# Masks by one whole number per column, stores on their makers' queues, first heads' values apart, output weights in four buffers, logs grouped

## Chip, cores, metric

One core of one Trainium2 chip runs the whole program. The metric is the device time of one execution in microseconds (us); the number compared is the median over several runs.

## What is computed

One layer of a hybrid encoder block on 1024 tokens of width 1024, all in float32:

```python
proj = h @ w_in[l]                                  # one projection for everything below
aq, ak, av, iq, ik, iw, bq, bk, bv, br, bg = split(proj)
# sparse attention, 8 heads of 64: an index score picks 256 keys per query
rel   = relu(einsum('bqhd,bsd->bqhs', iqb, ik))     # 8 index heads of 32
score = einsum('bqhs,bqh->bqs', rel, iwb)           # -inf for later chunks of 64
vals, idx = top_k(score, 256)                       # ties: the lower key first
p  = softmax(qb . k[idx] * 64**-0.5);  ya = p . v[idx]
# gated linear attention, 4 heads: decay from log_sigmoid(bg @ w_gate + b) / 16
log_a = log_sigmoid(bg @ w_gla_gate + b_gla_gate) / 16
b = cumsum(log_a) per chunk;  qg = q*exp(b);  kg = k*exp(-b);  ...
yb = rms_norm(o) * g * silu(br)
h = layer_norm(alpha*h + concat(ya, yb) @ w_out)
# mixture of 32 experts (4 groups of 8), top 2 inside the best group
h = layer_norm(alpha*h + hier_moe(h))
```

## The kernel before

Every float32 product is done as three products of rounded parts: a tensor x becomes `hi` (x rounded) and `lo` (x - hi), and TensorE (PE) sums hi*hi, hi*lo and lo*hi in PSUM. `split` makes the pair: ScalarE (ACT) copies `hi`, VectorE (DVE) or GpSimd (POOL) subtracts.

The work goes in stages. **Input phase** (`in_phase`): x^T is loaded and split into eight `big` tiles; index queries and keys and the first half of the attention's values (`values(0, ...)`) are projected, rotated and written to HBM scratch. `decays` makes the gates' logs: a matmul on the `g` PSUM banks, an exponential (L539), a logarithm with its subtraction (L542, L543), then a matmul with a triangle of ones that sums them (L547) and two exponentials of the sums, stored to `d_decay` (L552, L553). `index_scores` goes over query tiles t = 2 to 7 of 128 rows: for each of 8 index heads a matmul (L477), a Relu on ACT (L478) and a weighted accumulation on DVE (L484, L486). After each head it takes steps from `rest`, a generator of the linear attention's projections (`gla_inputs`); `BETWEEN` says how many units per head, one entry for each t. What is left of `rest` runs afterwards. A unit is one accumulation step (three matmuls) of a 256-column product; steps of a 512-column one count two.

**Queries and keys, threshold search, linear attention** run side by side. `queries_keys` projects (L221), rotates (DVE L264 to L267, POOL L268 and L269), splits (`split_out`) and stores queries and keys (`d_q`, `d_k`, L279 and L280). `topk_phase` finds the 256th largest score of each row by a search over the 31 bits of a float: four of the six columns (the query tiles 2 to 7, 384 to 1024 keys wide) are counted on DVE (L709), the two widest on ACT (L739). Then each column gets a mask in `bias`: the sign of score minus threshold (ACT L764), the ties (L765), a running count of them (L766), how many ties are still wanted (L768, L769), the wanted ties (L770), their sum with the sign on POOL (L771), and the comparison that writes 0 or -1e30 (L772). `values(1, ...)` projects the other half of the values at the end of this stage (L674 copies, L675 stores to `d_av`). `gla_phase` does the linear attention in four halves, stored through `ym` to `d_mix` (L664, L665).

**Attention** (`attention`): 32 items, four pairs of heads times eight query tiles, software-pipelined by hand: scores (L817), masked maximum (DVE L822), exponential (ACT L830), transposes (L841) copied to `PT` (L844, L846), product with the values (L855), normalization (POOL copy L888, transpose L863, L866) and store to `d_mix` (L867). `attention_loads` fetches queries, keys and values of a pair: for pair 0 into four tiles `kq0` to `kq3` of the pool `first_qk`, for the others into the `big` tiles that held x. Values of pairs 0 and 1 are loaded together into `kq3`, those of 2 and 3 into one `big` tile. At item 8 `first_qk` is closed, and the output weights' tiles `wolo`, `woraw`, `wohi` are opened over it: `load_wout` fetches a raw piece, `split_wout` splits it on POOL (L930, L931), one of 16 pieces after each of the items 8 to 23.

**Output projection** (`out_phase`): eight token tiles; each loads its mixed rows `mraw` (L1001; they share the `woraw` buffers) and the old x, multiplies by the split output weights (L1019), normalizes and routes. The first pieces of the experts' weights are loaded between (`next_raw`, L949). **Experts**: 32 experts in turn, 192 weight pieces of 1 MB streamed through 13 slots, split on ACT and DVE (L179, L180), multiplied (L1230), results added to `d_y` by an indirect DMA (L1279). A last normalization ends the kernel.

The order on each engine comes from the framework's scheduler, which plans with its own costs, except where `manual_schedule` or `issue_after` fixes it. Each engine runs its instructions in that order. A DMA is issued from a queue: SP's, ACT's or POOL's; the issue stands in that engine's order and waits there for what it needs. SP's queue carries nearly all DMAs.

Of the kernel before, what the change touches and what calls it, by code (L numbers as in the profile page):

```python
# [46 lines left out]
BETWEEN = (1, 1, 1.5, 1.5, 2, 2)  # L47
# [116 lines left out]
class Kern:  # L164
# [107 lines left out]
    def split_out(self, pool, src, dst_hi, dst_lo, lo_eng):  # L272

        nc = self.nc
        m, n = src.shape
        hi = pool.tile([128, 512], F32R, name="so_hi", bufs=2)[:m, :n]
        lo = src.bitcast(F32R)
        self.split(hi, lo, src, lo_eng)
        nc.sync.dma_start(dst_hi, hi.bitcast(F32))  # L279
        nc.sync.dma_start(dst_lo, lo.bitcast(F32))  # L280


    def run(self):
        tc, nc, I = self.tc, self.nc, self.I
        with ExitStack() as ctx:
# [34 lines left out]
            with ExitStack() as ps:  # L320
# [3 lines left out]
                with self.pool("att") as ap:  # L324
# [3 lines left out]
                    loads = [self.attention_loads(0, [fq.tile([128, 2, D], F32R if i < 3 else F32, name=f"kq{i}") for i in range(4)], nc.scalar)]  # L328

                    def more():  # L330
                        hp = len(loads)
                        loads.append(self.attention_loads(hp, [self.big(F32R) for _ in range(3)] + ([self.big()] if hp == 2 else [])))

                    def before(n):
# [3 lines left out]
                        if n == 8:  # L338
# [6 lines left out]
                            for q in range(2):  # L345
                                self.load_wout(wl, q)
# [19 lines left out]
    def in_phase(self, gla):  # L366
        tc, nc, I = self.tc, self.nc, self.I
        with ExitStack() as ctx:
# [6 lines left out]
            with self.pool("first") as fp:  # L375
# [23 lines left out]
                with self.pool("idx") as p:  # L399
# [10 lines left out]
                    self.decays(p)  # L410
# [4 lines left out]
                    self.index_scores(p, rest)  # L415
# [3 lines left out]
            with self.pool("qk") as p, self.pool("topk", side="right") as tp:  # L419
# [3 lines left out]
                self.all_of(self.values(1, self.load_w(I["wi"][P_AV + 1], 256), (0, 2, 4, 6)))  # L423
# [27 lines left out]
    def index_scores(self, p, rest):  # L451
# [13 lines left out]
        for t in range(2, NT):  # L465
            W = WS[t - 2]
# [54 lines left out]
    def decays(self, p):  # L521
# [7 lines left out]
        for hp, h in halves:  # L529
# [9 lines left out]
            nc.scalar.activation(u, u, AF.Exp)  # L539
            logs.append((u, loga))  # L540
        for u, loga in logs:
            nc.scalar.activation(u, u, AF.Ln, bias=1.0)  # L542
            nc.gpsimd.tensor_tensor(loga, loga, u, op=OP.subtract)  # L543
        for (hp, h), (u, loga) in zip(halves, logs):
# [4 lines left out]
            for k, tag in enumerate(("u", "loga")):  # L549
                e = p.tile([128, 512], F32, name=f"e{k}", tag=tag, bufs=4)  # L550

                nc.scalar.activation(e, bp, AF.Exp, scale=(0.0625, -0.0625)[k])  # L552
# [46 lines left out]
    def gla_half(self, p, hp, h, S, operands, AT, causal):  # L599
# [50 lines left out]
        for hd in range(2):  # L650
# [14 lines left out]
            nc.sync.dma_start(self.d_mix[h][:, :, 4 + 2 * hp + hd, :].rearrange("t p q -> p t q"), ym)  # L665
# [3 lines left out]
    def values(self, g, w, tiles):  # L669
        nc = self.nc  # L670
        for t in tiles:
# [3 lines left out]
            nc.sync.dma_start(self.d_av[g][:, :, t:t + 2, :].rearrange("a p t c -> p a t c"), vs)  # L675

    def queries_keys(self, p):
# [5 lines left out]
        for g in range(2):  # L683
            for n, dst in enumerate((self.d_q[g], self.d_k[g])):
                w = self.load_w(I["wi"][P_AQK + 2 * g + n], 256)
                for h in range(2):
# [4 lines left out]
                    for i in range(2):  # L691
                        o = dst[:, :, 32 * i:32 * i + 32, ts]
                        self.split_out(p, r[i], o[:, 0], o[:, 1], nc.gpsimd)


    def topk_phase(self, p):
# [4 lines left out]
        jnk = p.tile([128, T], BF, name="sn", bufs=1)  # L701
# [56 lines left out]
        for i in range(n):  # L758
            W = WS[i]

            sn = p.tile([128, T], BF, name="sn", bufs=1)[:, :W]
# [742 lines left out]
```

## Time and profile before

| | us |
|---|---|
| median of the 3 runs shown (1343.27 to 1349.84) | 1346.22 |
| the profiled execution's own time | 1340.77 |
| its span in the profile | 1339.0 |
| PE busy in the span | 1218.8 (91%) |
| DVE busy | 1016.0 (76%) |
| ACT busy | 801.1 (60%) |
| POOL busy | 385.5 (29%) |

Times in the profile count from the start of the span. Busy is the union of an engine's instructions. Matmuls overlap each other, so a busy PE is not always PE at its peak: many short ones at a low granted clock mean that it waits. The chain of waits is followed back from the last instruction; 67% of it lies on PE. "Idle before" an instruction names what ended the wait, by inference from semaphore events.

### The profile page before, as it was taken

The numbers are of one execution on the slowest core, as the hardware profiler recorded it, in microseconds if no ns is written. First come the engines' busy times: TensorE is split into PE (matmuls) and PEld (weight loads), VectorE is DVE, ScalarE is ACT, GpSimd is POOL, SyncE is SP. The second block draws the span as 40 slices with busy tenths as digits, with TensorE's granted clock in tenths as the row PEclk, the third lists the DMA queues.
The fourth block names the chain that finished last, engine by engine and source line by source line (L and its number), as shares of the span: only waits on it lengthen the run. The fifth ranks groups of instructions, "written<-read, shape, count | busy, mean of one in ns | idle before, by whom it ended". The sixth has DMA issues, their size and how long they took to land.

```text
span 1339.0 us, 19330 instructions
## 1 busy us (share of the span) xinstructions
PE 1218.8 (91%) x6894; PEld 1011.5 (76%) x6894; DVE 1016.0 (76%) x1646; ACT 801.1 (60%) x1117; POOL 385.5 (29%) x340
## 2 busy tenths in 40 slices
PE   7979999999994999499967999999999999999962
PEld 5967988977793887388856888888888888888841
DVE  4537888999854666256675999999999999999855
ACT  5487366665413666222244787777778777777735
POOL 3422532344652025411121212212222221222124
PEclk9988999999996999799968999999999999999985
DMA  7554434224366742567338999999999999999926
GB/s 250 160 166 139 127 127 141 95 74 143 110 192 181 204 111 65 211 231 260 138 112 314 335 371 371 382 375 368 366 367 373 354 354 350 358 357 347 352 55 251
DMA packets 130004, 322.57 MB, mean 241 GB/s; under 512 B 15577, under 2 KB 46194, under 8 KB 129906
## 3 DMA queue, kind: packets, MB, share of 16 engines
q1 hardware_dynamic: 114802, 287.73, 60.9%
q0 software_dynamic: 10496, 21.00, 6.1%
q10 hardware_dynamic: 4608, 12.58, 2.6%
q8 instruction: 55, 0.90, 0.3%
q14 instruction: 43, 0.35, 0.1%
HBM read 283.77 MB, written 54.26 MB: 252 GB/s over the span
## 4 chain that ended last, share of the span: by engine, by line
PE 67%; DMA 13%; DVE 9%; ACT 4%; issue 3%; POOL 2%; SPq 0%; ACTq 0%; POOLq 0%; DVEq 0%
PE acc L1230 23%; PE ot L1230 11%; PE acc L1019 7%; PE acc L235 6%; PE acc L221 4%; DVE eq L709 3%; PE pt L1293 3%; PE s L817 3%; PE ot L855 2%; DMA d_y<-y,tok 2%; PE pt L841 2%; DMA slot<-we 2%; PE g L221 2%; DMA big<-wf 2%; PE ot L1046 1%
## 5 line engine op out<-in xcount | busy, mean ns | idle before, releaser
L180 DVE TENSOR_TENSOR elo<-big,ehi 128x2048 fp32r<-128x2048 f32 (+1 forms) x132 | 268.1, 2061 | 22.2 <-ACT ehi L179 21.0
L179 ACT CAST ehi<-big 128x2048 fp32r<-128x2048 f32 (+1 forms) x132 | 223.1, 1724 | 3.8 <-DMA big<-we 2.5
L1230 PE MATMUL acc<-ehi,xh 128*128 128x512 f32 x512 | 206.5, 403 | 4.7 <-ACT sg L1342 4.7
L1230 PE MATMUL acc<-elo,xh 128*128 128x512 f32 x512 | 203.3, 397 | 0.3 <-DVE elo L180 0.3
L1230 PE MATMUL acc<-ehi,xl 128*128 128x512 f32 x512 | 203.2, 397 | 0.3 <-DVE xl L180 0.3
L1300 POOL DMA_INDIRECT xg<-d_h,tok x32 | 37.4, 1169 | 372.9 <-PE pt L1293 370.5
L235 PE MATMUL acc<-whi,big 128*128 128x256 f32 x736 | 136.5, 285 | 0.4 <-ACT rel L478 0.4
L221 PE MATMUL acc<-big,whi 128*128 128x512 f32 (+1 forms) x384 | 120.8, 394 | 9.7 <-ACT big L179 9.7
L1279 POOL DMA_INDIRECT d_y<-y,tok x32 | 92.8, 2900 | 100.5 <-DVE y L1278 40.6
L1230 PEld LDWEIGHTS acc<-ehi,xh 128*128 128x128 f32 x512 | 97.3, 190 | 26.5 <-ACT sg L1342 5.1
L235 PEld LDWEIGHTS acc<-whi,big 128*128 128x128 f32 x736 | 115.4, 191 | 2.4 <-issue 0.9
L1230 PEld LDWEIGHTS acc<-ehi,xl 128*128 128x128 f32 x512 | 97.1, 190 | 23.9 <-DVE xl L180 1.0
L1230 PEld LDWEIGHTS acc<-elo,xh 128*128 128x128 f32 x512 | 97.3, 190 | 22.5 <-DVE elo L180 1.2
L709 DVE TENSOR_SCALAR_CACHE_REDUCE eq<-sc,cand 128x384 bf16<-128x384 f32 (+1 forms) x124 | 100.5, 810 | 5.9 <-POOL sc L721 3.4
L235 PE MATMUL acc<-wlo,big 128*128 128x256 f32 x368 | 104.7, 285 | 0.0
L1230 PE MATMUL ot<-ehi,ah 128*128 128x512 f32 x256 | 103.6, 405 | 0.4 <-ACT ah L179 0.4
L180 DVE TENSOR_TENSOR elo<-slot,ehi 128x2048 fp32r<-128x2048 f32 (+1 forms) x46 | 95.5, 2101 | 9.5 <-ACT ehi L179 9.1
L1230 PE MATMUL ot<-ehi,al 128*128 128x512 f32 x256 | 101.1, 395 | 0.1
L1230 PE MATMUL ot<-elo,ah 128*128 128x512 f32 x256 | 101.0, 394 | 0.0
L1019 PE MATMUL acc<-wohi,m 128*128 128x512 f32 x256 | 84.1, 405 | 18.0 <-ACT m L179 18.0
L739 ACT ACTIVATE sn<-sc,cand 128x896 bf16<-128x896 f32 (+1 forms) x62 | 67.9, 1095 | 48.5 <-DVE cand L735 46.2
L221 PEld LDWEIGHTS acc<-big,whi 128*128 128x128 f32 x384 | 73.0, 194 | 25.5 <-ACT big L179 9.7
(288 smaller groups left out, 2565.5 us busy)
## 6 DMA issues: line engine op xcount, KB each, us to landing
big<-we SPq DMA_DIRECT2D x79, 1024.0 KB
big<-wf SPq DMA_DIRECT2D x40, 1024.0 KB
slot<-we SPq DMA_DIRECT2D x26, 1024.0 KB
sc<-we SPq DMA_DIRECT2D x20, 1024.0 KB
slot<-wf SPq DMA_DIRECT2D x16, 1024.0 KB
wraw<-wi SPq DMA_DIRECT2D x52, 256.0 KB
sc<-wf SPq DMA_DIRECT2D x8, 1024.0 KB
raw<-xT SPq DMA_DIRECT2D x8, 512.0 KB
```

The lines of the kernel that those rows point to most:

```text
L179: nc.scalar.copy(hi, src)
L180: (lo_eng or nc.vector).tensor_tensor(lo, src, hi.bitcast(F32), op=OP.subtract)
L221: nc.tensor.matmul(ps[:m, :n], l[:, j, c0:c0 + m], r[:, j % 2, t0:t0 + n], start=(j == 0 and a == 0), stop=(j == 7 and a == 2))
L235: nc.tensor.matmul(ps[:, i, :], l[:, j % 2, s], r[:, j, :], start=(j == 0 and a == 0), stop=(j == 7 and a == 2))
L709: nc.vector.tensor_scalar(gtt[:, :WS[i]], x, v, 0.0, op0=op, op1=OP.add, accum_out=cnt[:, i:i + 1])
L739: nc.scalar.activation(jnk[:, :WS[i]], y[i], AF.Sign, bias=c, accum_out=cnt[:, i:i + 1])
L817: nc.tensor.matmul(ps[:, 512 * c:512 * c + mm], lq, kk[hd][:, a, c0:c0 + mm], start=a == 0, stop=a == 1)
L1019: nc.tensor.matmul(ps, l[:, j, :], w[:, j, s], start=(j == 0 and a == 0), stop=(j == 7 and a == 2))
L1230: nc.tensor.matmul(o, x[:, jj, :], w[:, j, s], start=(jj == 0 and a == 0), stop=(jj == n - 1 and a == 2))
L1279: nc.gpsimd.indirect_dma_start(out=self.d_y, out_offset=bass.IndirectOffsetOnAxis(ap=tok.bitcast(U32), axis=0), in_=y, in_offset=None, bou ...
L1293: self.last_mm = nc.tensor.transpose(pt[:, 128 * i:128 * i + 128], src[:, 128 * (b + i):128 * (b + i) + 128], self.c["ident"])
L1300: self.last_gather = nc.gpsimd.indirect_dma_start(out=xg, out_offset=None, in_=self.d_h, in_offset=bass.IndirectOffsetOnAxis(ap=tok.bitcas ...
```

## The change

- **Masks.** Per column, DVE now forms 1024*sign - running count in the 16-bit float `pre` and compares it with one number per row, `need`, that says how many ties are taken. POOL's add goes. `sn` gets two buffers.
- **Stores.** In `queries_keys` the high part goes out from ACT's queue and the low part from POOL's; `values(1, ...)` and the linear attention's `ym` store from ACT's queue. All were on SP's.
- **First heads.** `attention_loads(0)` moves from ACT's queue to SP's. `kq3` holds the values of pair 0 alone and is half as large; pair 1 gets its values in a `big` tile of its own.
- **Output weights.** `woraw` has four buffers instead of two; the 16 pieces go by column half first and by row block second.
- **Logs.** `decays` ends after the logarithms, which are tied behind the last exponential on ACT; sums and their exponentials become `decay_sums`, called before query tile 5 in `index_scores` and tied behind the last logarithm. The last two entries of `BETWEEN` rise from 2 to 4.

```diff
-BETWEEN = (1, 1, 1.5, 1.5, 2, 2)
+BETWEEN = (1, 1, 1.5, 1.5, 4, 4)
+WORAW = 4
...
-    def split_out(self, pool, src, dst_hi, dst_lo, lo_eng):
+    def split_out(self, pool, src, dst_hi, dst_lo, lo_eng, queues=None):
...
-        nc.sync.dma_start(dst_hi, hi.bitcast(F32))
-        nc.sync.dma_start(dst_lo, lo.bitcast(F32))
+        q = queues or (nc.sync, nc.sync)
+        q[0].dma_start(dst_hi, hi.bitcast(F32))
+        q[1].dma_start(dst_lo, lo.bitcast(F32))
...
-                    loads = [self.attention_loads(0, [fq.tile([128, 2, D], F32R if i < 3 else F32, name=f"kq{i}") for i in range(4)], nc.scalar)]
+                    slots = [fq.tile([128, 2, D], F32R, name=f"kq{i}") for i in range(3)] + [fq.tile([128, D], F32, name="kq3")]
+                    loads = [self.attention_loads(0, slots)]
...
-                        loads.append(self.attention_loads(hp, [self.big(F32R) for _ in range(3)] + ([self.big()] if hp == 2 else [])))
+                        loads.append(self.attention_loads(hp, [self.big(F32R) for _ in range(3)] + ([self.big()[:, 0]] if hp == 1 else [self.big()] if hp == 2 else [])))
...
-                            for q in range(2):
+                            for q in range(WORAW):
                                 self.load_wout(wl, q)
...
-                    self.decays(p)
+                    logs = self.decays(p)
...
-                    self.index_scores(p, rest)
+                    self.index_scores(p, rest, lambda: self.decay_sums(p, *logs))
...
-                self.all_of(self.values(1, self.load_w(I["wi"][P_AV + 1], 256), (0, 2, 4, 6)))
+                self.all_of(self.values(1, self.load_w(I["wi"][P_AV + 1], 256), (0, 2, 4, 6), nc.scalar))
...
         for t in range(2, NT):
+            if t == 5:
+                between()
...
-            nc.scalar.activation(u, u, AF.Exp)
+            last = nc.scalar.activation(u, u, AF.Exp)
             logs.append((u, loga))
-        for u, loga in logs:
-            nc.scalar.activation(u, u, AF.Ln, bias=1.0)
-            nc.gpsimd.tensor_tensor(loga, loga, u, op=OP.subtract)
+        with self.tc.issue_after(last.ins):
+            for u, loga in logs:
+                last = nc.scalar.activation(u, u, AF.Ln, bias=1.0)
+                nc.gpsimd.tensor_tensor(loga, loga, u, op=OP.subtract)
+        return halves, logs, last
+
+    def decay_sums(self, p, halves, logs, last):
+        nc = self.nc
         for (hp, h), (u, loga) in zip(halves, logs):
...
-                nc.scalar.activation(e, bp, AF.Exp, scale=(0.0625, -0.0625)[k])
+                with self.tc.issue_after(last.ins):
+                    nc.scalar.activation(e, bp, AF.Exp, scale=(0.0625, -0.0625)[k])
...
-            nc.sync.dma_start(self.d_mix[h][:, :, 4 + 2 * hp + hd, :].rearrange("t p q -> p t q"), ym)
+            nc.scalar.dma_start(self.d_mix[h][:, :, 4 + 2 * hp + hd, :].rearrange("t p q -> p t q"), ym)
...
-                        self.split_out(p, r[i], o[:, 0], o[:, 1], nc.gpsimd)
+                        self.split_out(p, r[i], o[:, 0], o[:, 1], nc.gpsimd, (nc.scalar, nc.gpsimd))
...
-        jnk = p.tile([128, T], BF, name="sn", bufs=1)
+        jnk = p.tile([128, T], BF, name="sn", bufs=2)
...
-            sn = p.tile([128, T], BF, name="sn", bufs=1)[:, :W]
+            sn = p.tile([128, T], BF, name="sn", bufs=2)[:, :W]
...
+            nc.vector.tensor_scalar(need[:, i:i + 1], cnt[:, i:i + 1], 0.5, 0.5 * W - TOPK, op0=OP.mult, op1=OP.add)
             nc.vector.tensor_scalar(eq, sn, 0.0, None, op0=OP.is_equal)
             nc.vector.tensor_tensor_scan(pre, eq, eq, 0.0, op0=OP.add, op1=OP.max)
-            nc.vector.tensor_scalar(need[:, i:i + 1], cnt[:, i:i + 1], -0.5, TOPK - 0.5 * W, op0=OP.mult, op1=OP.add)
-            nc.vector.scalar_tensor_tensor(need[:, i:i + 1], pre[:, W - 1:W], 0.5, need[:, i:i + 1], op0=OP.mult, op1=OP.add)
-            nc.vector.scalar_tensor_tensor(eq, pre, need[:, i:i + 1], eq, op0=OP.is_le, op1=OP.mult)
-            nc.gpsimd.tensor_tensor(sn, sn, eq, op=OP.add)
-            nc.vector.tensor_scalar(self.bias[i + 2], sn, 0.0, NEG, op0=OP.is_le, op1=OP.mult)
+            nc.vector.scalar_tensor_tensor(need[:, i:i + 1], pre[:, W - 1:W], -0.5, need[:, i:i + 1], op0=OP.mult, op1=OP.add)
+            nc.vector.scalar_tensor_tensor(pre, sn, 1024.0, pre, op0=OP.mult, op1=OP.subtract)
+            nc.vector.tensor_scalar(self.bias[i + 2], pre, need[:, i:i + 1], NEG, op0=OP.is_lt, op1=OP.mult)
...
-    def attention_loads(self, hp, slots, queue=None):
+    def attention_loads(self, hp, slots):
...
-            if hp % 2 == 0:
-                queue.dma_start(self.vv.rearrange("p a (t c) -> p a t c", c=128)[:, :, 4 * th:4 * th + 4],
-                                  self.d_av[hp // 2][:, :, 4 * th:4 * th + 4].rearrange("a p t c -> p a t c"))
+            if hp < 2:
+                nc.sync.dma_start(self.vv.rearrange("p (t c) -> p t c", c=128)[:, 4 * th:4 * th + 4], d_av[hp][:, 4 * th:4 * th + 4])
...
-        raw = p.tile([128, 512], F32, name="woraw", tag="woraw", bufs=2)
-        s = slice(512 * (q % 2), 512 * (q % 2) + 512)
+        raw = p.tile([128, 512], F32, name="woraw", tag="woraw", bufs=WORAW)
+        s = slice(512 * (q // 8), 512 * (q // 8) + 512)
...
-        if q + 2 < 16:
-            self.load_wout(p, q + 2)
+        if q + WORAW < 16:
+            self.load_wout(p, q + WORAW)
...
-                raws = [self.wor.tile([128, 4, 128], F32, name="mraw", tag="woraw", bufs=2) for _ in range(2)]
+                raws = [self.wor.tile([128, 4, 128], F32, name="mraw", tag="woraw", bufs=WORAW) for _ in range(2)]
```

More of the change, by code (lines that the diff above doesn't have):

```diff
@@ L449, in index_keys, with index_scores @@
             self.split_out(p, r[i], dk[i, :, ts], dk[2 + i, :, ts], nc.vector)
-    def index_scores(self, p, rest):
+    def index_scores(self, p, rest, between):
         nc, I = self.nc, self.I
@@ L664, in gla_half, with values @@
             nc.scalar.copy(ym.rearrange("p a b -> p (a b)"), tps)
-            nc.sync.dma_start(self.d_mix[h][:, :, 4 + 2 * hp + hd, :].rearrange("t p q -> p t q"), ym)
+            nc.scalar.dma_start(self.d_mix[h][:, :, 4 + 2 * hp + hd, :].rearrange("t p q -> p t q"), ym)
         return S
-    def values(self, g, w, tiles):
+    def values(self, g, w, tiles, queue=None):
         nc = self.nc
+        queue = queue or nc.sync
         for t in tiles:
@@ L674, in values @@
             nc.scalar.copy(vs, ps.rearrange("p t (a b) -> p a t b", a=2))
-            nc.sync.dma_start(self.d_av[g][:, :, t:t + 2, :].rearrange("a p t c -> p a t c"), vs)
+            queue.dma_start(self.d_av[g][:, :, t:t + 2, :].rearrange("a p t c -> p a t c"), vs)
     def queries_keys(self, p):
@@ L775, in topk_phase @@
         nc.vector.tensor_copy(self.bias[1][:, 128:256], self.c["diag"])
-    def attention_loads(self, hp, slots, queue=None):
-        queue = queue or self.nc.sync
-        d_q, d_k, h0 = self.d_q[hp // 2], self.d_k[hp // 2], 2 * (hp % 2)
+    def attention_loads(self, hp, slots):
+        nc = self.nc
+        d_q, d_k, d_av, h0 = self.d_q[hp // 2], self.d_k[hp // 2], self.d_av[hp // 2], 2 * (hp % 2)
         qq, kk = slots[0], slots[1:3]
-        if hp % 2 == 0:
+        if len(slots) > 3:
             self.vv = slots[3]
@@ L919, in load_wout @@
     def load_wout(self, p, q):
[L921 to L923 removed]
+        raw = p.tile([128, 512], F32, name="woraw", tag="woraw", bufs=WORAW)
+        s = slice(512 * (q // 8), 512 * (q // 8) + 512)
+        self.nc.gpsimd.dma_start(raw, self.I["wo"].rearrange("(j p) c -> p j c", p=128)[:, q % 8, s])
         self.woraw.append(raw)
     def split_wout(self, p, q):
[L927 to L928 removed]
+        s = slice(512 * (q // 8), 512 * (q // 8) + 512)
+        hi, lo = self.wohi[:, q % 8, s], self.wolo[:, q % 8, s]
         raw = self.woraw[q]
```

16 lines of the change are left out of this document (8 added, 8 removed).

## Prediction

> **What bounds the kernel now.** I read the page first: TensorE (PE) is the busiest engine by far, so a part beside a full PE can pay nothing. I then cut the span into stages (busy time of each engine by window) to find where PE stands still, and read each engine's timeline, the list of waits and the chain of waits around those places.
>
> ```profile
> 70.00:85.00 15.00, 7.85 (x37) 6.39 (x35) 0.18 (x1) 14.50 (x23) 6.45 (x6) 0.66 0.36 122
> 85.00:119.00 34.00, 33.91 (x178) 29.51 (x179) 22.68 (x29) 22.94 (x49) 7.62 (x8) 1.00 0.49 146
> 119.00:137.40 18.40, 16.52 (x40) 8.38 (x38) 17.15 (x17) 15.66 (x33) 1.70 (x4) 0.72 0.49 151
> 137.40:407.00 269.60, 266.83 (x1818) 232.40 (x1818) 228.86 (x619) 139.20 (x295) 126.22 (x107) 0.99 0.40 127
> 407.00:430.20 23.20, 4.65 (x18) 3.42 (x18) 7.23 (x25) 5.32 (x14) 5.00 (x3) 0.54 0.72 194
> 430.20:548.20 118.00, 113.78 (x1071) 94.95 (x1070) 71.01 (x180) 76.89 (x174) 34.62 (x46) 0.99 0.46 124
> 548.20:566.20 18.00, 0.04 (x1) 0.04 (x1) 0.75 (x2) 1.20 (x2) 8.38 (x10) 0.61 0.90 332
> ...
> 726.00:1275.00 549.00, 548.82 (x2543) 448.42 (x2544) 497.98 (x348) 413.36 (x346) 118.00 (x59) 1.00 0.99 359
> ```
>
> Columns: window, its length, busy time of PE, PE's weight loads, VectorE (DVE), ScalarE (ACT) and GpSimd (POOL) with instruction counts, granted clock, DMA share, GB/s. Four windows have a hole: 70 to 85 (the gate logs), 7.2 us without PE work and a clock of 0.66; 119 to 137.4 (the last two index-score tiles), where 40 matmuls spread over 16.5 us at 0.72; 407 to 430.2 (start of the attention), 4.65 busy of 23.2; 548.2 to 566.2 (start of the output projection), 0.04 of 18.0. Between them PE is full: 266.83 of 269.6 us from 137.4, 548.82 of 549 in the experts. The change can win in these holes only.
>
> **Hole 1: the logs.**
>
> ACT's timeline (start us, length us, line, operation), and PE's row, whose bracket is the idle time before it:
>
> ```profile
> 61.89 1.28 ACT L542 ACT_TABLE_LOAD   x1
> 63.19 0.63 ACT L542 ACTIVATE u<-u 128x512 f32<-128x512 f32 x1
> ...
> 75.49 1.28 ACT L552 ACT_TABLE_LOAD   x1
> 76.79 1.08 ACT L552 ACTIVATE e<-g 128x512 f32<-128x512 f32 x2
> ```
>
> ```profile
> 77.97 2.05 PE L547 MATMUL g<-Kin,loga 128*128 128x128 f32 x8 [6.23 <-issue]
> ```
>
> ACT alternates exponential and logarithm with a table load of 1.28 us each time: eight from 61.89 to 75.49. PE stands 6.23 us until the last sums of the logs. The change ties all logarithms behind the last exponential and the later exponentials behind the last logarithm: two loads, six fewer, 6 x 1.28 = 7.7 us of ACT. It also puts the sums (four groups of eight matmuls, eight exponentials of 0.54 us, their stores) behind the third index tile, so no score queues behind them. PE gets back 7.2 us, and of the 7.85 us busy at clock 0.66 some 2 to 3 us. Against that, 8 x 0.54 + 1.28 = 5.6 us of ACT move into the score stage. ACT has 11 of 34 us free from 85 to 119, which hides them; in the last two tiles it has 2.7 us free, and then up to 5.6 us show. I take 8 gained, ends 3 and 10.
>
> ScalarE: Activation LUTs of the Trainium skill, "Table sets: the hidden batching unit", says that exponential and logarithm lie together in one set, so that going from one to the other needs no second load. By that rule grouping would save no load, and the sum would be 36 us instead of 44; the trace does not agree, it has a load of 1.28 us at each alternation.
>
> **Hole 2: the last score tiles.**
>
> PE's timeline, and a window in which it runs 256-column matmuls almost alone:
>
> ```profile
> 119.43 1.73 PE L477 MATMUL acc<-K,Q 128*128 128x384 f32 x6
> ...
> 128.23 8.76 PE L477 MATMUL acc<-K,Q 128*128 128x512 f32 x16 [0.36 <-ACT rel L478]
> ```
>
> ```profile
> 154.00:180.00 26.00, 26.00 (x212) 25.70 (x211) 21.63 (x56) 13.36 (x24) 20.34 (x15) 1.00 0.47 148
> ```
>
> These rows are the first and last of the stretch in which PE holds scores alone. Its matmuls need at most 0.23 us each at full clock (512 columns, twice the 256 below), 7 to 8 us; about 11 are unused. DVE (17.15 of 18.4) and ACT (15.66) pace it. The raised last entries of BETWEEN feed two more projection steps after each of 16 heads: 32 steps of three 256-column matmuls at 26.0/212 = 0.123 us, together 11.8 us. This work leaves the full stretch after 137.4 and fits the hole. It brings two more copies and some weight casts on ACT, about 5 x 0.6 = 3 us, which can stretch a stage that ACT and DVE pace. Ends: 11 gained, 3 lost. I take 8, nearer the fill, because 85 to 119 ran the same mixture at 33.91 of 34.
>
> Together PE ends its projections 16 us sooner, at about 390.
>
> **Hole 3: the attention's start.**
>
> The waits from 345 to 432 (us in total, times, longest), the chain, and the timelines of SP's queue, PE, ACT and DVE:
>
> ```profile
> ACT vs L674 <- DMA d_av<-vs: 14.7, 2, 10.6
> ...
> PE s L817 <- ACT vs L674: 11.2, 1, 11.2
> ...
> DVE sc L772 <- POOL sn L771: 3.4, 3, 2.2
> ```
>
> ```profile
> 410.60 11.40 DMA d_av<-vs
> ```
>
> ```profile
> 422.70 0.38 SPq L675 DMA_DIRECT2D d_av<-vs  x1
> ```
>
> ```profile
> 418.03 1.22 PE L817 MATMUL s<-kq,kq 128*128 128x256 f32 x4 [11.17 <-ACT vs L674]
> ```
>
> ```profile
> 425.05 0.27 ACT L846 COPY PT<-pt 128x128 f32<-128x128 f32 x1 [0.18 <-PE pt L841]
> ```
>
> ```profile
> 352.12 0.17 DVE L757 SCALAR_TENSOR_TENSOR v<-thr,sg 128x6 f32<-128x6 f32 x1
> ...
> 405.32 2.29 DVE L766 TENSOR_TENSOR_SCAN pre<-eq 128x1024 f16<-128x1024 bf16 x1
> ...
> 413.20 0.43 DVE L772 TENSOR_SCALAR sc<-sn 128x1024 bf16<-128x1024 bf16 x1 [2.23 <-POOL sn L771]
> ...
> 429.15 0.29 DVE L844 COPY PT<-pt 128x128 f32<-128x128 f32 x1 [3.24 <-DMA big<-d_k]
> ```
>
> PE's first score is done at 406.9 (418.03 less 11.17 of idle time). ACT's value copies then wait 10.6 and 4.1 us for the landing of their own stores, which stand in SP's queue behind the query and key stores; the score banks wait for the copies, and the first tile that DVE turns waits 3.24 us more, for the last of those stores (issued 422.70, released 429.15: 6.5 us). The change gives the value stores to ACT's queue, behind the copies themselves, the query and key stores to ACT's (high part) and POOL's (low part), and the first heads' loads, which stood on ACT, to SP. What remains: the chain from the second score to the first turned copy, 418.03 to 425.05 = 7.0 us, beside the last value store's landing (0.5 issue, 4.1 to 6.5 landing), and the copy, 0.6. I leave 9 of 23.2: 14 gained. Ends: 16 (the 7 us chain alone), and 6 (the store lands after 11.4 us, as in the chain's row, with some 6 us around it).
>
> The masks lie beside this. Each of six columns loses POOL's add, for which DVE waited 3.4 us in all, keeps six DVE operations, and ACT may run one column ahead. Today the last mask is written at 413.20, but behind the queues above. Alone, the widest column needs DVE for two passes at no more than the scan's 2.29, two at 0.43 and short ones, 6 us; six columns of 0.69 of that width on average 25 us. From thresholds now at 352.1, perhaps 7 sooner, the masks end near 370: neither gain nor cost, since PE ends at 390. If the new comparison, with a pointer scalar and a 16-bit float, ran at the scan's pace, 6 x 1.86 = 11 us more still fit.
>
> The issues that write one tensor (min/median/max ns):
>
> ```profile
> L279 SPq DMA_DIRECT2D d_q<-so_hi x8: 516/524/587, 297.8 to 375.6; - x8
> ```
>
> The queues take on 28 stores on ACT (16 high parts, 4 values, 8 of the linear attention) at 0.52 us, 14.6 us, less 16 loads that leave it; 16 on POOL at 0.56 us (a row below) are 9 us. ACT is busy for 139 and POOL for 126 of 269.6 us there, so this is hidden; if the cover went, these 15 and 9 us would show.
>
> **Hole 4: the output projection's start.**
>
> The views of the raw output weights and of the first pair's tiles, PE's timeline, and the chain:
>
> ```profile
> L923 POOL DMA_DIRECT2D woraw<-wo x16: 546/563/836, 489.5 to 553.8; - x16
> L930 POOL CAST wohi<-woraw x16: 609/613/617, 492.8 to 560.8; 128x512 fp32r<-128x512 f32 x16
> L931 POOL TENSOR_TENSOR wolo<-woraw,wohi x16: 1256/1268/1288, 495.5 to 562.6; 128x512 fp32r<-128x512 f32 x16
> ...
>   DMA woraw<-wo: 20.8, 9
> ...
> DMA to landing us min/median/max: 2.9/3.2/6.1
> ```
>
> ```profile
> L855 PE MATMUL ot<-PT,kq x288: 272/273/476, 430.2 to 488.9; 128*64 128x128 f32 x144
> ```
>
> ```profile
> 457.27 1.97 PE L855 MATMUL ot<-PT,kq 128*64 128x128 f32 x32
> ```
>
> ```profile
> 562.70 2.69 DMA mraw<-d_mix
> 565.49 0.63 ACT m L179
> ```
>
> POOL splits the output weights: 16 x (0.56 + 0.61 + 1.27) = 39 us and 20.8 us of waiting for two buffers. It starts at 489.5, because the region that it overlays holds the values of head pairs 0 and 1, last used at 488.9. It ends at 562.7, and the mixed rows, which share those buffers, load only then. In the change that region holds pair 0 alone, done at 459.2: the splits start 30 us sooner and with four buffers lose most of the 20.8. At worst 459.7 + 39 + 20.8 + 5 for POOL's small copies between = 525 on today's clock, 23 us ahead of the attention's end. POOL's splits beside the attention cost PE nothing today (113.78 of 118). Late next are the rows' load (2.69) and cast (0.63) after the attention's tiles are free at about 548.2: 552 instead of 566.2. I take 14 gained; ends 16 (rows loaded before), and 8 (1 MB weight loads issued at that moment delay the rows by 6). The weights' order by column halves only helps the first products. Pair 3's queries now wait for pair 1's slot, free by 488.9, instead of a spare one; a pair takes 30 us, so they are used at about 519: hidden.
>
> **Sum.** 8 + 8 + 14 + 14 = 44 us. The profiled execution's own time is 1340.77 (span 1339.0, 1.8 around it): 1296.8. The median of the shown runs, 1346.22, is 5.5 above it: 1302 on their scale. I put 1300. The ends add up to gains of 14 to 53 us.
>
> **Rivals.**
>
> *Landing, not queueing, holds the attention (0.15).* The last value store is still awaited and shares the DMA engines with the loads of pairs 0 and 1. For it: a DMA share of 0.72 there, and 11.40 us in the chain. Against it: one store instead of a backlog. Hole 3 then gives 6: 1308.
>
> *The threshold search becomes the bound (0.20).* DVE is busy for 228.86 of 269.6 us with one serial search in it. With PE 16 us ahead, masks may end after PE. Only what starts the search sooner, 5 to 8 us, then remains of holes 1 and 2: 1309. Against it: the mask chain loses POOL, and the third tile needs only the first column.
>
> *The expert stream swallows hole 4 (0.08).*
>
> The chain near its end:
>
> ```profile
> 1219.96 21.83 DMA big<-wf
> 1241.79 23.31 DMA slot<-we
> ```
>
> It runs through weight loads of 22 and 23 us, and the DMA share is 0.99. Were the stream tied to a fixed start, 14 us would come back as waits: 1314. Against it: the early weights are issued between the output tiles and move with them.
>
> *POOL's queue makes it slower (0.06).* Sixteen stores stand in POOL's order among the additions that finish each rotation. If each held POOL, the rotation's buffers and then PE's banks would fill. It outweighs the 44 us from 44/16 = 2.75 us per store; at a whole landing each, 3.2 to 6.1 us by the tile's row, it costs 51 to 98: 1351 to 1398. Against it: issues of 0.546 to 0.836 us beside a busy DVE; no row before has a store on POOL's queue. SBUF — State Buffer of the Trainium skill, "A bandwidth-pool intuition that's wrong", gives a mechanism: POOL cannot write descriptors while VectorE holds the shared port, and 620 ns became 3100. An estimate from these figures, 16 x 2.48 = 40 us, would leave 1340; the issue rows do not show it.
>
> **How the numbers follow.** All four holes pay: 0.51, its own range 1288 to 1317. With the rivals at 1308, 1309, 1314 and above 1351, eight in ten lie in 1284 to 1328; the top takes in the small ends (14 to 17 gained), the bottom the large ones. A measurement of this kernel tells some 0.5% (6.7 us) from no change. Slower is the POOL rival, 0.06; about the same, several small ends together, 0.04; faster 0.90.
>
> **What would show it.** Right: two table loads between the gate and the first score, no PE hole there; scores (L477) with projections between them up to the last tile; under 10 us of PE hole before the attention, with value copies that wait for no store; splits done long before the last head, and the first output matmul within 6 us of the attention's end. Wrong: masks as the releaser of the first scores, POOL held by its own issues, or mixed rows loaded late for another reason.

## The result: 3.2% less time, with the third hole only partly closed

The changed kernel takes 1304.14 us (median of 4 runs, 1301.16 to 1305.77), the kernel before 1345.86 (4 runs): a ratio of 0.9685, 95% interval 0.9655 to 0.9715. A second series beside the experiments gave 0.9710 (0.9687 to 0.9733). The profiled execution took 1303.8 us, 37.0 less than the profiled one before.

Stage windows of the changed kernel (columns as in the prediction):

```profile
70.00:85.00 15.00, 13.99 (x67) 11.89 (x68) 10.53 (x11) 10.28 (x22) 10.82 (x9) 1.00 0.45 120
85.00:110.00 25.00, 23.72 (x133) 20.22 (x132) 14.85 (x18) 20.27 (x47) 4.01 (x5) 1.00 0.55 168
110.00:131.40 21.40, 21.40 (x155) 20.60 (x155) 19.85 (x17) 18.50 (x38) 4.94 (x6) 1.00 0.36 103
131.40:393.90 262.50, 255.38 (x1723) 221.48 (x1722) 233.89 (x621) 137.44 (x292) 131.60 (x118) 0.98 0.46 136
393.90:411.10 17.20, 4.08 (x19) 3.29 (x18) 2.69 (x21) 5.88 (x15) 0.89 (x2) 0.60 0.78 228
411.10:527.30 116.20, 112.02 (x1068) 93.71 (x1068) 71.41 (x180) 76.75 (x173) 42.59 (x56) 1.00 0.51 149
527.30:529.10 1.80, 0.61 (x7) 0.37 (x5) 0.55 (x1) 1.17 (x3) 0.00 (x0) 1.00 0.00 0
```

All four holes are smaller. From 70 to 85 TensorE (PE) is busy for 13.99 us at full clock, where it was 7.85 at 0.66. From 110 to 131.4, with the last score tiles, it has no gap. The output projection follows the attention after 1.8 us instead of 18.0. But 393.9 to 411.1, between the projections and the attention's first value matmul, still holds 17.2 us with 4.08 of work, and the long stretch before it, which lacked 2.8 of 269.6 us, now lacks 7.1 of 262.5.

Taken as gains along the profiled execution: the projections end 12.7 us sooner (406.5 to 393.85), the gap behind them gives 6.4, the attention itself 1.8, the gap behind it 16.2. That is the 37. (The profiled execution before lay 5 us under its median; between the medians it is 41.7.)

ScalarE (ACT) before the attention, then PE (the bracket is the idle time before an instruction and what ended it):

```profile
388.98 0.62 ACT L180 CAST so_hi<-rp 128x512 fp32r<-128x512 f32 x1 [9.76 <-DMA d_k<-so_hi]
...
391.47 0.62 ACT L180 CAST so_hi<-rp 128x512 fp32r<-128x512 f32 x1 [1.87 <-DMA d_k<-so_hi]
...
392.69 0.59 ACT L686 COPY vs<-acc 128x512 f32<-128x512 f32 x1 [0.60 <-PE acc L236]
...
402.85 0.58 ACT L686 COPY vs<-acc 128x512 f32<-128x512 f32 x1 [8.55 <-DMA d_av<-vs]
...
405.24 0.58 ACT L686 COPY vs<-acc 128x512 f32<-128x512 f32 x1 [1.81 <-DMA d_av<-vs]
...
406.25 1.28 ACT L848 ACT_TABLE_LOAD   x1 [0.43 <-ACT vs L686]
407.55 0.40 ACT L848 ACTIVATE Sm<-Sm,mx 128x128 f32<-128x128 f32 x1
```

```profile
393.85 0.63 PE L835 MATMUL s<-kq,kq 128*128 128x256 f32 x4
...
408.10 0.47 PE L859 MATMUL pt<-K,Sm 128*128 128x128 f32 x1 [12.96 <-ACT Sm L848]
...
411.12 0.44 PE L873 MATMUL ot<-PT,kq 128*64 128x128 f32 x4
```

ACT works its queue in order. It casts the high halves of two keys late, because it waits for the landing of its own earlier key stores (9.76 and 1.87 us); the third and fourth value copy wait 8.55 and 1.81 us for the first two value stores, since there are two buffers. Only then come the table load and the first exponential, and PE waits 12.96 us for it. These lines answer to the 10.6 and 4.1 us of value copies in the profile before: the stores moved to another queue, and a wait of 8.55 and 1.81 us for their landing stayed.

### The profile page after: what moved, and what is told of

The parts are those of the page before. It is cut to its first block, busy times and chain, and to the rows that moved or that the text cites. A ratio compares the mean times of both kernels' runs of the same rounds, so it can differ in the third digit from the quotient of the medians.

```text
span 1302.0 us, 19312 instructions
## 1 busy us (share of the span) xinstructions
PE 1204.9 (93%) x6894; PEld 1006.3 (77%) x6894; DVE 1021.8 (78%) x1646; ACT 792.0 (61%) x1111; POOL 386.1 (30%) x350
## 4 chain that ended last, share of the span: by engine, by line
PE 69%; DMA 12%; DVE 9%; ACT 5%; issue 3%; POOL 2%; SPq 0%; ACTq 0%; POOLq 0%; DVEq 0%
PE acc L1248 24%; PE ot L1248 12%; PE acc L1037 7%; PE acc L236 5%; PE acc L222 4%; DMA big<-we 3%; PE s L835 3%; PE ot L873 3%; PE pt L1311 3%; DVE eq L722 3%; DMA d_y<-y,tok 2%; PE pt L859 2%; PE g L236 1%; DMA extra<-we 1%; DMA d_mix<-ym 1%
## 5 line engine op out<-in xcount | busy, mean ns | idle before, releaser
L236 PE MATMUL acc<-whi,big 128*128 128x256 f32 x672 | 126.3, 287 | 0.0
L1297 POOL DMA_INDIRECT d_y<-y,tok x32 | 89.5, 2797 | 106.3 <-DVE y L1296 46.0
L236 PEld LDWEIGHTS acc<-whi,big 128*128 128x128 f32 x672 | 106.3, 193 | 1.9 <-issue 1.2
L236 PE MATMUL acc<-wlo,big 128*128 128x256 f32 x336 | 96.2, 286 | 0.0
```

Source lines behind the costliest of these rows:

```text
L236: nc.tensor.matmul(ps[:, i, :], l[:, j % 2, s], r[:, j, :], start=(j == 0 and a == 0), stop=(j == 7 and a == 2))
L1297: nc.gpsimd.indirect_dma_start(out=self.d_y, out_offset=bass.IndirectOffsetOnAxis(ap=tok.bitcast(U32), axis=0), in_=y, in_offset=None, bou ...
```

## The experiments

Each kernel ran five or six times beside the kernel before ("changed" is the result above). The table gives its ratio to that kernel, and from its profile the starts (us) of the last projection matmul, the last mask, the first value matmul of the attention and the first output matmul.

| kernel | ratio (95%) | projections | masks | values | output |
|---|---|---|---|---|---|
| before | 1 | 406.3 | 413.2 | 430.2 | 566.2 |
| changed | 0.9685 (0.9655-0.9715) | 393.7 | 387.3 | 411.1 | 529.1 |
| after_again | 0.9710 (0.9687-0.9733) | 392.8 | 389.6 | 410.4 | 529.3 |
| u_out | 0.9825 (0.9802-0.9848) | 393.9 | 388.0 | 410.0 | 546.1 |
| u_logs | 0.9872 (0.9850-0.9894) | 411.4 | 394.8 | 439.8 | 558.6 |
| u_between | 0.9836 (0.9813-0.9860) | 409.9 | 389.9 | 427.0 | 545.0 |
| b_logs | 0.9854 (0.9830-0.9878) | 389.3 | 404.3 | 413.3 | 549.7 |
| u_queues | 0.9785 (0.9762-0.9807) | 388.7 | 376.9 | 416.6 | 536.9 |
| u_masks | 0.9760 (0.9737-0.9784) | 394.4 | 416.5 | 421.0 | 539.0 |
| ym_sp | 0.9678 (0.9653-0.9703) | 391.3 | 380.9 | 411.5 | 530.3 |
| vs4 | 0.9692 (0.9672-0.9712) | 392.4 | 386.5 | 407.4 | 525.6 |
| vsp | 0.9678 (0.9653-0.9702) | 392.1 | 388.2 | 406.2 | 526.3 |
| vsp2 | 0.9613 (0.9587-0.9639) | 393.7 | 390.5 | 402.6 | 521.1 |
| vsp2_noact | 0.9608 (0.9583-0.9633) | 393.8 | 387.2 | 400.0 | 518.5 |

Below, a ratio is compared with 0.970, the mean of the changed kernel's two; 0.001 is 1.3 us, and differences under some 0.003 are not told apart.

> The changed kernel as it is, beside the others on this chip: 0.9685 of the kernel before, 1300 us where the kernel before takes 1343.

It came out at 0.9710, 1304.82 us where the kernel before takes 1343.56; the two intervals overlap.

### Parts undone, or added alone

**u_out: the output side.**

```
-WORAW = 4
+WORAW = 2
-... + [fq.tile([128, D], F32, name="kq3")]
+... + [fq.tile([128, 2, D], F32, name="kq3")]   # values of pairs 0 and 1 together
```

> The changed kernel with the two output-side edits undone: two raw buffers for the output weights again, and the first two head pairs' values shared in one wide tile. Theory (the four holes add): the first output matmul, now 1.8 us behind the attention's end, goes back to 18 us behind it, and all after it moves with it: 1304 + 16 = 1320 us (1317 to 1323). Rival (the experts' weights are the bound behind the output projection): the experts absorb part of the delay, the first expert matmul moves by less than the first output matmul, and the time is under 1313 us.

The order of the weight pieces stays the changed one here, and pair 1 has no value tile of its own. Measured: 17 us more (0.9825 against 0.970), all of it between the attention's end and the first output matmul (546.1 against 529.1). GpSimd's weight splits, tile view of u_out, then of the changed kernel:

```profile
L947 POOL TENSOR_TENSOR wolo<-woraw,wohi x16: 1257/1270/1287, 473.7 to 542.8; 128x512 fp32r<-128x512 f32 x16
...
  DMA woraw<-wo: 18.3, 11
```

```profile
L941 POOL DMA_DIRECT2D woraw<-wo x16: 546/550/613, 433.1 to 495.8; - x16
...
L949 POOL TENSOR_TENSOR wolo<-woraw,wohi x16: 1265/1278/1298, 446.0 to 508.9; 128x512 fp32r<-128x512 f32 x16
...
  DMA woraw<-wo: 4.3, 4
```

Undone, the last split starts at 542.8 and GpSimd stands 18.3 us for raw buffers; in the changed kernel it starts at 508.9 with 4.3 us of standing, and PE goes on at once:

```profile
527.24 0.66 PE L881 MATMUL pt<-K,rb 128*128 128x128 f32 x4
529.09 0.50 PE L1037 MATMUL acc<-wohi,m 128*128 128x512 f32 x1 [1.19 <-ACT m L180]
```

The theory holds. Which of the two edits does how much was not separated.

**u_logs and u_between: the logs and the fill.** u_logs takes back both, u_between only the last two entries:

```
-BETWEEN = (1, 1, 1.5, 1.5, 4, 4)
+BETWEEN = (1, 1, 1.5, 1.5, 2, 2)
```

> The changed kernel with the logs ungrouped (logarithms straight behind the exponentials by the scheduler's choice, decay sums in place) and 2, 2 instead of 4, 4 projection steps between the last score tiles. Theory (TensorE is the bound up to the last projection): the holes of 8 and 8 us at 70 to 85 and 119 to 137 come back, the last projection ends 10 to 13 us later than at 393.85 and the time is 1304 + 12 = 1316 us (1313 to 1319). Rival (the threshold search on VectorE is the bound of that stretch: the last threshold was ready at 354.61, not earlier than before's 352.12): the projections end less than 5 us later, and the time is under 1309 us.

> The changed kernel with 2, 2 projection steps in place of 4, 4 between the last score tiles, the logs still grouped. Theory (hole 2 is its own 8 us): half of what u_logs cost at the end of the projections (411.4 against 393.7) comes back, they end at 400 to 403, and the time is 7 to 9 us above the changed kernel's. Rival (the grouping of the logs pays for both holes: with the sums moved behind the fifth score tile the last score tiles have their work anyway): under 3 us.

u_logs costs 17.7 us at the projections' end, more than the 10 to 13 of the theory (the rival allowed 5), and 23 us in time, where the theory had 12: the start of the attention grew as well, 411.4 to 439.8. (Its profiled execution lay 6 us above its median.) The list of waits from 390 to 440 names the value copies, which wait for their stores:

```profile
PE s L827 <- ACT vs L678: 15.4, 1, 15.4
```

u_between costs 16.2 us at that end and 18 in time, twice the theory's 8, with the logs still grouped. Its windows (120 to 130 and 280 to 320), ACT and PE:

```profile
120.00:130.00 10.00, 9.15 (x18) 4.47 (x18) 9.48 (x9) 8.73 (x18) 1.07 (x3) 0.66 0.51 168
280.00:320.00 40.00, 32.11 (x160) 25.78 (x159) 30.10 (x80) 20.93 (x46) 20.44 (x20) 0.83 0.34 91
```

```profile
291.65 0.37 ACTq L676 DMA_DIRECT2D d_mix<-ym  x1
...
305.21 0.58 ACT L675 COPY ym<-g 128x512 f32<-128x512 f32 x1 [8.49 <-DMA d_mix<-ym]
```

```profile
305.85 2.07 PE L622 MATMUL g<-qg,kg 64*128 64x128 f32 x8 [7.89 <-ACT ym L675]
```

The hole among the last score tiles is back (18 matmuls in 10 us, clock 0.66); then ACT's second store of that half finds its single buffer held by the first, issued 291.65 and released 13.6 us later, and PE waits 7.89 us for the copy. In the changed kernel the window 280 to 320 has 39.21 busy at clock 0.96, and PE waits for such copies 2.3 us in all. How the 16 us divide can be estimated. Both kernels end the scores at about the same time (last score matmul at 130.2 and 131.4), and behind them u_between has 912 matmuls of the 256-column kind left, the changed kernel 816: 96 more at the prediction's 0.123 us are 11.8 us, which is hole 2. The other 4 are what is left of the stall, and of the clock of 0.83 beside it, after the changed kernel's own waits.

**b_logs: the logs' part alone, put into the kernel before.**

> The kernel before with the logs' part of the change alone: logarithms grouped, decay sums behind the fourth score tile, 4, 4 projection steps between the last score tiles. Theory (TensorE is the bound up to the last projection, and the parts add): the projections end at about 390 instead of 406.3, the attention starts 16 us sooner, and the time is 1344 - 16 = 1328 us (1325 to 1331). Rival (in the kernel before the start of the attention hangs on the stores behind SyncE's queue and on the masks, ready at 413, and not on the projections' end): the projections end 16 us sooner, but the first value matmul moves from 430 to 420 at best, and the time is 1334 us or more.

The projections end 17.0 us sooner, the first value matmul comes 16.9 sooner, and the time falls by 19.6 (0.9854 of 1345; 15.6 between the profiled executions). The theory holds, though the sums stand behind the third score tile and not the fourth. The attention then starts at 413.3 with the old masks and the old queues, only 2 us behind the changed kernel. What holds it there is not the value copies but the first masked maxima on VectorE (DVE), which stand behind the old masks:

```profile
PE s L825 <- DVE mx L830: 14.7, 1, 14.7
```

**u_queues and ym_sp: the stores.** u_queues puts every store on SyncE's (SP's) queue again and the first pair's loads on ACT's, ym_sp moves only the stores of the linear attention:

```
-nc.scalar.dma_start(self.d_mix[h][:, :, 4 + 2 * hp + hd, :]..., ym)
+nc.sync.dma_start(self.d_mix[h][:, :, 4 + 2 * hp + hd, :]..., ym)
```

> The changed kernel with all stores on SyncE's queue again and the first pair's attention loads on ScalarE's. Theory (queueing was part of the third hole): the gap between the last projection and the first value matmul goes from 17 back to 23 us, the other stretches stay: 1304 + 6 = 1310 us (1307 to 1313). Rival A (landing alone holds the copies, whichever queue issues the store): within 2 us of the changed kernel, 1302 to 1306 us. Rival B (ScalarE held by the landings of its own stores costs more than SyncE's queue did): the 6 us that TensorE loses between 200 and 350 us come back too, and the time is 1300 us or less.

> The changed kernel with the eight stores of the linear-attention outputs alone back on SyncE's queue. With all stores there (u_queues) the last threshold was ready at 343.1 instead of 354.6 and the projections ended at 388.7 instead of 393.7. Theory (those stores on ScalarE's queue hold the sign counts behind them, and the threshold search with them): the thresholds come at about 345 and the projections end at about 389; the time falls by 5 us or less, as ScalarE then waits longer for the key stores ahead of the value copies. Rival (the query and key stores on ScalarE's queue do it): threshold and projections stay within 2 us of the changed kernel's, and so does the time.

u_queues is 11 us slower, more than the 6 expected, and in two opposite parts: its projections end 5 us sooner, but the gap behind them is 27.9 instead of 17.4 us, with one wait of ACT:

```profile
386.87 1.07 ACT L686 COPY vs<-acc 128x512 f32<-128x512 f32 x2
404.96 1.26 ACT L686 COPY vs<-acc 128x512 f32<-128x512 f32 x2 [17.02 <-DMA d_av<-vs]
```

So beside the new masks the queues were worth 10.5 us at the attention's start, and the projections ended 5 us later with them. ym_sp shows the thresholds at 345.4 instead of 354.6, as the theory said, but the projections' end moves by 1.5 to 2.4 us only, the attention starts at 411.5, and the time (0.9678) is not told apart from the changed kernel's: the thresholds are not what PE waits for.

**u_masks: the former masks.** (The front of this document has the diff.)

> The changed kernel with the masks built the former way (the comparison with the ranks multiplied by the ties, an addition on GpSimd, then the comparison with zero), with one sign buffer. Theory (the masks run beside the second group's projections, ending at 387.3, ahead of TensorE's end at 393.7): the last mask comes at 400 to 410, after the projections, but no item of the attention needs it before; within 3 us of the changed kernel. Rival (VectorE and GpSimd are nearly the bound there: the query and key splits on GpSimd wait behind the additions): the projections or the key stores come later, and the time is 6 us or more above the changed kernel's.

The rival's size came out, by neither mechanism: projections within 2 us, 8 us more in time, lost at the attention's start. DVE, then PE:

```profile
416.51 0.43 DVE L786 TENSOR_SCALAR sc<-sn 128x1024 bf16<-128x1024 bf16 x1 [2.29 <-POOL sn L785]
```

```profile
417.20 0.80 PE L835 MATMUL s<-kq,kq 128*128 128x256 f32 x2 [18.97 <-DVE mx L840]
```

The first item's second score waits 18.97 us for DVE. No item needs the last mask yet, but DVE works in order, and the last mask, 416.51, stands ahead of the masked maxima that empty the score banks.

Taken together, the starts of the attention (one profiled execution each) say that the masks and the queues pay only as a pair. The first value matmul comes at 413.3 with both old (b_logs), at 416.6 with new masks and old queues, at 421.0 with new queues and old masks, and at 411.1 with both new. (b_logs lacks the output side too, but u_out shows that this does not move the start: 410.0.) In time the logs (19.6) and the output side (17) come to 37 of the 41 us, which leaves some 4 for the pair; the pair was not added alone.

### What holds the third hole

**vs4: buffers for the third and fourth value copy.**

```
+            if free and t > 2:
+                vs = free.tile(..., tag=f"rp{t // 2}", bufs=1)
```

> The changed kernel with one thing added: the third and fourth value tiles of the second group get buffers of their own (idle ones of the rotation's temporaries), so that their copies do not wait for the first two tiles' stores to land. Theory (the rest of the third hole is the rotation through two buffers, 8.55 + 1.81 us on ScalarE): the four copies follow one another from 392.7, the first exponential starts at about 397 instead of 407.55, and the time is 1304 - 10 = 1294 us (1292 to 1297). Rival (the transfer engines are full there, and the first pair's operands or the second pair's loads hold the attention instead): TensorE's hole shifts to a wait for a load, and the time stays above 1300 us.

ACT in vs4:

```profile
392.66 0.37 ACTq L690 DMA_DIRECT2D d_av<-vs  x1
...
395.66 0.59 ACT L689 COPY vs<-acc 128x512 f32<-128x512 f32 x1 [0.92 <-ACT vs L689]
401.97 0.37 ACTq L690 DMA_DIRECT2D d_av<-vs  x1
402.37 1.28 ACT L851 ACT_TABLE_LOAD   x1 [6.12 <-DMA d_av<-vs]
```

The copies follow one another to 396.2, but the fourth *store* is issued at 401.97. The trace shows why. The transfers of SP's and ACT's queues carry eight completion counters (semaphores) between them, in turn, and those of GpSimd's queue eight others. First and fourth value store have the same one; ACT waits on it ahead of the fourth, and the last part of the first store landed at 401.89. The value matmul comes 3 to 4 us sooner; in time (1301.1 us, 0.9692) this is not told apart, so the theory's 10 us did not come.

**vsp: the four value stores on GpSimd's queue as well,** which has counters of its own.

> The changed kernel with buffers of their own for the third and fourth value tiles and the four value stores on GpSimd's queue. With the buffers alone ScalarE's fourth store was issued only at 401.97, 6.12 us late: in the compiled program the transfers of SyncE's and ScalarE's queues signal eight completion counters in turn, and that issue waits for the first value store, which has the same counter; GpSimd's queue has eight of its own. Theory (ScalarE is held by its own stores, by whichever of buffers and counters): with no store to issue it copies all four tiles by 395, the first exponential starts at about 396 instead of 407.55, the hole between the last projection and the first value matmul shrinks from 17 to 6 us, and the time is 11 us below the changed kernel's. Rival (the transfers themselves hold the start: operands of the first pair, or something else than ScalarE): another wait of 6 us or more takes the place, and the time is less than 5 us below.

ACT, then DVE:

```profile
393.39 2.05 ACT L689 COPY vs<-acc 128x512 f32<-128x512 f32 x4 [0.60 <-ACT so_hi L180]
395.46 1.28 ACT L851 ACT_TABLE_LOAD   x1
```

```profile
405.13 0.29 DVE L865 COPY PT<-pt 128x128 f32<-128x128 f32 x1 [6.45 <-DMA d_av<-vs]
```

ACT is free at 395.46, 11 us sooner. But now DVE's first copy of transposed weights waits 6.45 us, for a value store: its tile lies at the address of the first two value tiles, still being read by their stores. (Ahead of that copy DVE waits on the counters of just these two stores; the second landed at 405.05.) The rival's wait of 6 us came, by a third form of the same landing, and 3 us in time, not told apart.

**vsp2: all four value tiles where the attention does not write at first.**

```
+            if free and t < 4:
+                vs = free.tile(..., tag=f"rp{2 + t // 2}", bufs=1)
+            elif free:
+                vs = self.sA[:, 512 * (t // 2 - 2):512 * (t // 2 - 1)]...
```

> As vsp (value stores on GpSimd's queue), with all four value tiles in places that the attention does not write in its first items: two of the rotation's temporaries and the two halves of the sine table. In vsp ScalarE was free at 395.46, but VectorE's first copy of transposed weights waited until 405.13 for a value store: its tile lies where the first two value tiles had been. Theory (the hole is the landing of the value stores, seen through buffers, counters and reused space, and through nothing else): the first value matmul comes at about 399.5 instead of 410.7, and the time is 11 us below the changed kernel's, ratio 0.961 to 0.964. Rival (the second pair's loads, issued from 390 to 408 behind shared completion counters, are late next): the start moves, but TensorE waits as long at the eighth item of the attention, and the ratio stays above 0.966.

ACT, then PE:

```profile
391.74 0.62 ACT L180 CAST so_hi<-rp 128x512 fp32r<-128x512 f32 x1 [9.28 <-DMA d_k<-so_hi]
...
396.51 1.09 ACT L691 COPY sA<-acc 128x512 f32<-128x512 f32 x2
397.62 1.28 ACT L853 ACT_TABLE_LOAD   x1
```

```profile
399.46 0.47 PE L864 MATMUL pt<-K,Sm 128*128 128x128 f32 x1 [2.53 <-ACT Sm L853]
...
402.64 0.70 PE L878 MATMUL ot<-PT,kq 128*64 128x128 f32 x4
```

The first value matmul starts at 402.6 instead of 410.4 to 411.1 and the time is 12 us below the changed kernel's, ratio 0.9613: the landing of the value stores, through buffers, counters and reused space, was 8.5 of the 17.4 us of this hole, and 8.9 are left. 3 us of the expected start are missing, since ACT still waits for key stores before its key casts (391.74).

**vsp2_noact: no store left on ACT's queue.**

```
-..., nc.gpsimd, (nc.scalar, nc.gpsimd))
+..., nc.gpsimd, (nc.gpsimd, nc.gpsimd))
```

> As vsp2, with no store left on ScalarE's queue: the linear attention's outputs on SyncE's, the high halves of queries and keys on GpSimd's beside the low ones. Theory (ScalarE's own stores cost TensorE the 4 to 5 us by which the projections ended sooner in u_queues, 388.7 against 393.7): the projections end at 389 to 390 and the time is 3 to 5 us below vsp2's. Rival (GpSimd, busy 27 of 40 us there, now issues sixteen stores at 0.70 us, or SyncE's queue holds the outputs): the projections end where vsp2's do or later, and the time is vsp2's or up to 4 us more.

The projections end where vsp2's do, as the rival says; the attention starts 2.6 us sooner, as those casts no longer wait for key stores. 0.9608 against 0.9613 is no difference that can be told. Why u_queues and b_logs end their projections at 389 and the others at 391 to 394 stays open in part. Windows of vsp2, then of vsp2_noact:

```profile
200.00:240.00 40.00, 36.91 (x309) 33.14 (x310) 33.54 (x107) 23.44 (x55) 10.91 (x12) 0.91 0.38 112
```

```profile
200.00:240.00 40.00, 39.87 (x363) 36.11 (x362) 35.18 (x121) 29.21 (x70) 11.29 (x14) 1.00 0.46 139
280.00:320.00 40.00, 38.38 (x198) 29.95 (x197) 39.35 (x102) 19.25 (x35) 26.46 (x28) 0.91 0.52 121
```

Without stores on ACT, PE fills the stretch from 200 to 240 as it does in u_queues (39.61) and ym_sp (39.53), so the linear attention's stores did cost it there. What this won was lost elsewhere, to the clock above all. An estimate from the windows from 60 to 394 (the missing share of the clock times the length) has 9 us lost in vsp2_noact, a part of it before 85, ahead of everything that the edit moves; 5 in vsp2 and in the changed kernel; none in u_queues. Each is one execution. That GpSimd issues no stores in u_queues and b_logs was not tried by itself.

## Why the prediction was right, point by point

The time was forecast as 1300 and is 1304. The sum said 44 us, and 37.0 came in the profiled execution (41.7 between the medians): hole 3 gave 7.6 less, the projections' end 3.3 less, hole 4 gave 2.2 more, and the attention 1.8 that no step had. So 10.9 us too much was partly made up by 4.0 too little; that the time came within 4 us of the forecast is in part luck. The mechanism held for three holes of four, and failed for the third and for the masks.

**Holes 1 and 2 (8 + 8, PE's projections at 390).** Right: the part alone ends them at 389.3, and moves the time by 19.6 us. ACT of the changed kernel between the gate and the first decay sums:

```profile
67.57 1.28 ACT L548 ACT_TABLE_LOAD   x1
68.87 2.19 ACT L548 ACTIVATE u<-u 128x512 f32<-128x512 f32 x4
...
84.69 1.28 ACT L563 ACT_TABLE_LOAD   x1
85.98 1.08 ACT L563 ACTIVATE e<-g 128x512 f32<-128x512 f32 x2
```

Two table loads of 1.28 us, as forecast, and PE is busy for 13.99 of the 15 us. The Trainium skill (ScalarE: Activation LUTs, "Table sets: the hidden batching unit") has both functions in one set, by which nothing would be saved; the trace has a load at each change of function. Taken apart, each term came out above its 8 where it arises: grouping without the fill ends the scores 9 us sooner (last score matmul at 130.2 instead of 139.2) with the same projections left, and the fill is worth 11.8 us by the estimate above. Only 1.5 of the 9 us reach the projections' end in u_between (411.4 to 409.9); its stall of 7.89 us on a store takes most of the rest. In the changed kernel, too, the stretch behind the scores gives some back: 7.1 us without PE work where it was 2.8. A slip in the step changes little: twice 0.123 us is 0.246, not 0.23, so that nearer 10 than 11 us were unused.

**The stores' price (15 us of issues on ACT, 9 on GpSimd, hidden).** The wrong price. GpSimd's issues took 0.70 to 0.73 us in the median, tile rows of its stores:

```profile
L282 POOL DMA_DIRECT2D d_q<-rp x8: 688/728/1006, 286.5 to 366.6; - x8
L282 POOL DMA_DIRECT2D d_k<-rp x8: 688/704/713, 312.6 to 394.1; - x8
```

The POOL rival's mechanism (the Trainium skill, SBUF — State Buffer, "A bandwidth-pool intuition that's wrong") would have shown here as issues of 3 us; the trace does not agree, since the longest took 1.01. What cost time was not the issue but the landing: ACT standing still for buffers of its own stores, and PE with it (36.66 busy from 200 to 240, where u_queues has 39.61). How much of the 4.4 us by which the projections end later than with the logs alone (393.7, 389.3) is this and how much the clock stays open.

**Hole 3 (14 of 23.2, 9 left).** The mis-sized term: 17.2 are left. "The change gives the value stores to ACT's queue" was followed as if the queue were the whole wait; it was a part (10.5 us by u_queues), and the landing another (8.5 by vsp2). The row that the step quoted, 10.6 us of ACT for d_av<-vs with 11.40 of landing in the chain, already said that the copies wait for landings; the claim of "value copies that wait for no store" had no row behind it. This is the rival "Landing, not queueing", given 0.15: it forecast 6 us for this hole, and 6.4 came.

**The masks (neither gain nor cost).** Wrong. "Perhaps 7 sooner" for the thresholds failed:

```profile
354.61 1.22 DVE L770 SCALAR_TENSOR_TENSOR v<-thr,sg 128x6 f32<-128x6 f32 x1
```

They came 2.5 us later than before, held by ACT's stores (ym_sp: 345.4), and the masks ended at 388 instead of near 370. Still the edit pays 8 us, because the old masks would end at 416.5 in a queue that the first scores share. The threshold rival had DVE as the bound of PE; ym_sp excludes it for the changed kernel, while with the old masks DVE does hold the first scores (u_masks, b_logs).

**Hole 4 (14).** Right in mechanism and a little small: 16.2 in the profile, 17 by u_out. GpSimd got the first pair's region at 439.3, where the forecast has 459.2 on the old clock; the attention had started 19.1 us sooner, so this is as forecast. The splits ended at 510; the 525 of the step, moved by as much, is 506. The mixed rows were issued at 519.1, before the attention's end: the case of the end of 16. The expert stream gave nothing back: from the first output matmul to the end of the span it is 772.9 us, and was 772.8.

## What to carry to other kernels

A store that leaves its queue sooner still has to land: when a copy waits for a store, look at how long the landing takes and at everything that the landing holds (the tile's buffer, a completion counter shared by other queues, the address that a later tile takes) and free all of them, since vs4 and vsp, which freed one and two, gained 3 us at most, and vsp2, which freed all three, gained 12. Value the parts of a change both alone and by undoing them: the parts undone here add up to 17 + 23 + 11 + 8 = 59 us, and the whole is 41. Masks and queues cost 8 and 11 us when one is undone, yet with logs and output side in place some 4 us are left for both together, since each helps only beside the other. And an engine that works in order delays its first urgent instruction by whatever stands ahead, needed or not.

## What was not expected

A 256 KB store, issued in 0.37 us, held what it read for 9.5 us with the DMA engines 0.86 busy (393.30 to 402.85, changed kernel), and for 13.6 us with 0.49 busy (291.65 to 305.21, u_between). The best version measured, vsp2_noact, takes 1290.57 us, 0.9608 of the kernel before; vsp2 is not told apart from it.
